# Matmul steps of 512 + 256 columns become three products of 256 columns, but for the opening step of each output block

## The chip, the cores and the metric

The kernel runs on one core of a Trainium2 chip. The metric is the device time of one execution in microseconds (us), as the median of several runs. The profile is one execution of its own, recorded by the hardware profiler.

## The reference

One layer of a streaming encoder over a sequence of 256 tokens of width 2048, all in float32. Every large product in it has the 256 tokens on one side and a weight matrix on the other:

```python
u = rms_norm(h, norm_mix[l])
proj = u @ w_in[l]
...
h = h + jnp.concatenate([o_dn.astype(h.dtype), o_mla.astype(h.dtype)], axis=-1) @ w_out[l]
h = h + memory_cross_attention(rms_norm(h, norm_xattn[l]), mem_n, xa_wq[l],
                               xa_wk[l], xa_wv[l], xa_wo[l])
h = h + conv_ffn(rms_norm(h, norm_ffn[l]), ffn_w_up[l], ffn_conv[l],
                 ffn_conv_bias[l], ffn_w_down[l])
```

`w_in` feeds a delta-rule head group and a latent-attention head group; `w_up` has 2 x 5632 columns, `w_down` 5632 rows. A final normalisation follows.

## The kernel before

Activations lie with features on the 128 partitions and the 256 tokens (T = 256) along the free axis. To keep float32 accuracy with the cheaper `fp32r` matmul, each operand is split into a high and a low part. An activation tile holds `[x_hi | x_lo]` side by side in 512 columns; a weight tile is loaded by DMA (`raw`), ScalarE writes its high part `wh` (L102) and VectorE the low part `wl` (L103). One k step adds to a block of 128 output features what 128 input features give: `wh·x_hi`, `wh·x_lo` and `wl·x_hi`.

`kstep` (L116 to L122) makes a k step of two matmuls: `wh` by all 512 columns into a whole PSUM bank (L122), so that `wh·x_lo` collects in columns 256 to 511, and `wl` by 256 columns into the lower half (L120). Every other step turns the two around, so that the stream on TensorE reads 512, 256, 256, 512, 512, 256, 256, 512 and so on. When a block is done, `halves` (L140, L141) or `add_res` adds the two halves of the bank.

`kstep3` (L125 to L127) makes the same step of three matmuls of 256 columns, all into the lower half. It serves the query projection of the cross-attention (`xa_wq`, tile `xq`), the block products of the latent attention (tile `lath`), the scores and mixes of the cross-attention (tiles `kh`, `qh`, `pTx`, in the PSUM tiles `psa` and `psb`), and the last block of `w_down`. The change leaves it as it is.

`kstep` makes 3460 k steps. By the tile that it reads:

- `u`: 39 blocks of 16 steps of the input projection (the first in the program);
- `om` and `od`: the two halves of the output projection, 16 blocks of 8 steps each;
- `mh`: 16 blocks of 16 steps for the keys of the cross-attention;
- `xo`: 16 blocks of 16 steps of its output projection;
- `fx`: 88 blocks of 16 steps of `w_up`;
- `ga` and `gb`: 15 blocks of 44 steps of `w_down` (a sixteenth is made with `kstep3`).

In the first 406 us `fill(n)` draws n steps of `u` or `om` at a time between the small float32 matmuls of the two attention groups. From `od` on, the blocks follow one another on TensorE with few other matmuls between them (`rstd_col` and `rstd_row`, the `v_block` of 512-column products, scores and mixes). TensorE's order is that of the code; the other engines are ordered by a scheduler.

Of the kernel before, what the change touches and what calls it, by code (L numbers as in the profile page):

```python
# [22 lines left out]
T = 256  # L23
# [47 lines left out]
def trunk(ctx, tc, a):  # L71
    nc = tc.nc
    V, S, PE = nc.vector, nc.scalar, nc.tensor
# [8 lines left out]
    def psg():  # L82
        return pg.tile([P, 512], F32, name="psg", tag="psg")

    def psa(tag="a"):
        return pa.tile([P, 512], F32, name="ps" + tag, tag=tag, bufs=1 if tag == "c" else 2)
# [19 lines left out]
    def load_w(src, n=1024, pieces=1):  # L106
        raw = wpool.tile([P, 1024], F32, name="raw", tag="raw")
        nc.sync.dma_start(raw[:, 0:n], src)
        return split_w(raw, n, pieces)

    turn_ = [False]

    def kstep(ps, wh, wl, xh2, first, last):
        rev = turn_[0] and not first  # L116
        turn_[0] = not rev
        for lo in ((True, False) if rev else (False, True)):
            if lo:
                PE.matmul(ps[:, 0:256], wl, xh2[:, 0:256], start=False, stop=last, skip_group_check=True)  # L120
            else:
                PE.matmul(ps[:, 0:512], wh, xh2, start=first, stop=last, skip_group_check=True)  # L122

    def kstep3(ps, wh, wl, xh2, first, last):
        PE.matmul(ps[:, 0:T], wh, xh2[:, 0:T], start=first, stop=False)  # L125
# [3 lines left out]
    def gemm_block(w, nb, x, step=kstep):  # L129
        ps = psg()  # L130
        for hf in range(2):
            wh, wl = load_w(w[2 * nb + hf])
            for j in range(8):
                k = 8 * hf + j
                step(ps, wh[:, j * P:(j + 1) * P], wl[:, j * P:(j + 1) * P], x(k), k == 0, k == KC - 1)
        return ps
# [29 lines left out]


    def rstd_col(*accs):
        ps = psa("c")
        for t in range(2):  # L170
            for i, acc in enumerate(accs):
                PE.matmul(ps[:, t:t + 1], acc[:, t * P:(t + 1) * P], ones[:, 0:1], start=i == 0,
                          stop=i == len(accs) - 1)
        r = small.tile([P, 2], F32, name="rcol", tag="rcol", bufs=2)
        S.activation(r, ps[:, 0:2], AF.Sqrt, scale=1.0 / D, bias=eps)
        V.reciprocal(r, r)
        return r

    def rstd_row(col):
        ps = psa("c")  # L180
        for t in range(2):
            PE.matmul(ps[:, t * P:(t + 1) * P], col[:, t:t + 1].to_broadcast([P, P]), idn, start=True, stop=True)
        r = small.tile([P, T], F32, name="rrow", tag="rstd", bufs=2)
        S.copy(r, ps[:, 0:T])
        return r
# [4 lines left out]
    with ExitStack() as ph:  # L190
# [11 lines left out]
        with tc.tile_pool(name="xpool", bufs=1) as xpl:  # L202
# [13 lines left out]
            for k in range(KC):  # L216
                wh, wl = w0[k // 8]
                j = k % 8
                kstep(ps0, wh[:, j * P:(j + 1) * P], wl[:, j * P:(j + 1) * P], u(k), k == 0, k == KC - 1)
# [49 lines left out]
        def drawn():  # L269
            ready = {0: lead}  # L270
            ps = None
            i = 0
            while i < len(queue):
                for n in range(i, min(i + 1 + ahead[0], len(queue))):
                    if n not in ready:
                        ready[n] = load_w(queue[n][0], pieces=2)
                _, x, begin, first, last, done = queue[i]
                if begin:
                    begin()
                wh, wl = ready.pop(i)  # L280
                if first:
                    ps = psg()
                for j in range(8):
                    kstep(ps, wh[:, j * P:(j + 1) * P], wl[:, j * P:(j + 1) * P], x(j),
                          first and j == 0, last and j == 7)
                    if last and j == 7:
                        done(ps)
                    pos[0] += 1
                    for at_, f in [t for t in later if t[0] <= pos[0]]:
                        later.remove((at_, f))  # L290
                        f()
                    yield
                i += 1
# [3 lines left out]
        gen = drawn()  # L297

        def fill(n):
            for _ in range(n):  # L300
                next(gen, None)

        def until(n):
            fill(n - pos[0])
# [66 lines left out]
        with ExitStack() as ms:  # L371
# [20 lines left out]

            lats.append(latent)
            fill(8)
            rs0 = rstd_col(*accs)
            fill(6)
            rs.append(rstd_row(rs0))
            latent(0, ps0)
            latent(1, ps1)
            until(Q0 + 8)  # L400
            ps = psa()
# [72 lines left out]
            ps = psa()  # L474
# [5 lines left out]
            ps = psa()  # L480
# [22 lines left out]
            def w_mla(i):  # L503
                c = order.index(i)
                for n in order[c:c + 2]:
                    if n not in wm:
                        wm[n] = load_w(a["w_mla"][n])
                return wm[i]
# [63 lines left out]
            for i in range(2):  # L572
                kn = mp.tile([P, 4, T], F32, name="kn", tag="kn")
                wh, wl = w_mla(i)
                for n in range(4):
                    ps = psg()
# [8 lines left out]
                wh, wl = w_mla(2 + i)  # L585
                for t in range(2):
                    ps = psg()
# [325 lines left out]
    with ExitStack() as ph:  # L913
# [4 lines left out]
        for n in range(KC):  # L918
            wh, wl = load_w(a["w_out"][2 * n + 1])
            ps = psg()  # L920
# [15 lines left out]
        for n in range(KC):  # L936
            ps = gemm_block(a["xa_wk"], n, mh)
            if n == 0:
                rmc = rstd_col(macc)
                psk = ps  # L940
            else:
                if n == 1:
                    rsm = rstd_row(rmc)
                    normed(psk, rsm, kT[:, 0])
                normed(ps, rsm, kT[:, n])
            split_gain(xq(n), hT[:, n], sm[:, C_XA + n:C_XA + n + 1])
            accum_sq(xacc, hT[:, n], n == 0)
# [80 lines left out]
        for n in range(3):  # L1028
            v_block(n)
            if n == 0:  # L1030
                rcx = rstd_col(xacc)
            elif n == 1:
                rsx = rstd_row(rcx)
# [23 lines left out]
        for n in range(KC):  # L1057
            if n < 3:
                ps = pw[n]
            else:  # L1060
                ps = psg()
# [10 lines left out]
    with ExitStack() as ph:  # L1072
# [39 lines left out]
        for n in range(KC):  # L1112
            ps = psg()
            for c in range(6):
                nk = 8 if c < 5 else 4
                o = n * NF * P + c * 1024
                wh, wl = load_w(a["w_down"][n, :, c * 1024:c * 1024 + nk * P], nk * P)
# [131 lines left out]
```

## Time and profile before

| what | value |
| --- | --- |
| median of 3 runs | 1580.1 us (1579.47 to 1580.53) |
| time of the profiled execution | 1580.7 us |
| its span in the trace | 1578.9 us |
| TensorE (PE) busy | 1546.1 us, 98% of the span |
| weight loads (PEld), which overlap PE | 1358.5 us, 86% |
| VectorE (DVE) busy | 1119.3 us, 71% |
| ScalarE (ACT) busy | 889.3 us, 56% |
| DMA | mean 179 GB/s |

The profiled execution's time is its span and 1.8 us around it. Matmuls overlap: a 256-column matmul is shown as lasting 0.28 us, but the next starts after some 0.11 to 0.12 us. The price of a matmul in a stream is therefore the distance from its start to the next start, not its duration.

### The profile page before, as it was taken

To read this page: it belongs to the slowest core of one execution; us is meant where nothing else is said; L and a number is where in the kernel's file an instruction comes from. 1 tells how busy PE (TensorE), PEld (TensorE's weight loads), DVE (VectorE), ACT (ScalarE), POOL (GpSimd) and SP (SyncE) were. 2 spreads that over 40 slices of the span, in tenths; PEclk is the share of its full clock that TensorE was granted. 3 is DMA by queue.
4 is the path that set the end of the run, shared out by engine and by line. 5 is a ranking of instruction groups with operands and counts; after the bars stand their busy time and mean duration, and the time that the engine had idled before them with its cause. 6 is when DMAs were issued, how large, how long until landed. Compare 5 with 4: busy or idle time off the path is not lost.

```text
span 1578.9 us, 24577 instructions
## 1 busy us (share of the span) xinstructions
PE 1546.1 (98%) x9386; PEld 1358.5 (86%) x9386; DVE 1119.3 (71%) x1810; ACT 889.3 (56%) x1473; POOL 147.9 (9%) x152
## 2 busy tenths in 40 slices
PE   7999999999999999999999999999999999999996
PEld 5887877888888889999888888888888888888886
DVE  8687688696976555566777888878888886445453
ACT  7867666757764444455556666556665665344441
POOL 2224021001320000000110000000000000111112
PEclk9999999999999999999999999999999999999998
DMA  7564443364665555544555555555555556666663
GB/s 248 179 214 141 144 134 126 118 214 132 200 200 189 191 188 193 174 161 133 174 188 187 187 189 190 194 188 189 192 193 187 187 190 183 190 190 183 198 187 106
DMA packets 80773, 282.22 MB, mean 179 GB/s; under 512 B 9392, under 2 KB 10304, under 8 KB 80656
## 3 DMA queue, kind: packets, MB, share of 16 engines
q1 hardware_dynamic: 79344, 277.86, 54.3%
q0 software_dynamic: 1312, 2.80, 0.6%
q8 instruction: 73, 1.20, 0.3%
q14 instruction: 44, 0.36, 0.1%
HBM read 277.83 MB, written 2.11 MB: 177 GB/s over the span
## 4 chain that ended last, share of the span: by engine, by line
PE 88%; DVE 5%; ACT 4%; issue 1%; DMA 1%; SPq 0%; DVEq 0%; ACTq 0%
PE psg L122 46%; PE psg L120 23%; PE psg L125 3%; PE psg L126 3%; PE psg L127 3%; PE psg L960 2%; PE psg L959 2%; PE psg L958 2%; DVE wl L103 2%; ACT wh L102 1%; DMA raw<-in_w_out_dram 1%; PE psa L620 0%; PE psa L539 0%; DVE qkv L330 0%; DVE hT L1132 0%
## 5 line engine op out<-in xcount | busy, mean ns | idle before, releaser
L103 DVE TENSOR_TENSOR wl<-raw,wh 128x1024 fp32r<-128x1024 f32 (+2 forms) x614 | 647.3, 1061 | 286.1 <-ACT wh L102 279.2
L102 ACT CAST wh<-raw 128x1024 fp32r<-128x1024 f32 (+2 forms) x614 | 550.8, 909 | 401.5 <-PE psg L122 243.2
L122 PE MATMUL psg<-fx,wh 128*128 128x512 f32 x1408 | 439.8, 393 | 0.0
L120 PEld LDWEIGHTS psg<-fx,wl 128*128 128x128 f32 x1408 | 264.7, 188 | 60.0
L120 PE MATMUL psg<-fx,wl 128*128 128x256 f32 x1408 | 277.6, 279 | 0.0
L122 PE MATMUL psg<-u,wh 128*128 128x512 f32 x624 | 207.7, 404 | 8.9 <-DVE u L149 8.2
L122 PEld LDWEIGHTS psg<-fx,wh 128*128 128x128 f32 x1408 | 212.0, 188 | 0.0
L120 PEld LDWEIGHTS psg<-u,wl 128*128 128x128 f32 x624 | 119.3, 192 | 29.3 <-DVE wl L103 3.1
L140 ACT COPY half<-psg 128x256 f32<-128x256 f32 x143 | 53.2, 372 | 154.9 <-PE psg L122 154.7
L120 PE MATMUL psg<-u,wl 128*128 128x256 f32 x624 | 134.3, 289 | 1.7 <-DVE wl L103 1.7
L122 PE MATMUL psg<-gb,wh 128*128 128x512 f32 x420 | 133.4, 393 | 0.0
L122 PEld LDWEIGHTS psg<-u,wh 128*128 128x128 f32 x624 | 99.3, 191 | 12.5 <-DVE u L149 9.0
L120 PEld LDWEIGHTS psg<-gb,wl 128*128 128x128 f32 x420 | 79.0, 188 | 17.9
L1089 DVE SCALAR_TENSOR_TENSOR y<-ub,sm,y 128x256 f32<-128x256 f32 x176 | 84.7, 482 | 3.5 <-ACT y L1087 0.3
L120 PE MATMUL psg<-gb,wl 128*128 128x256 f32 x420 | 82.8, 278 | 0.0
L122 PE MATMUL psg<-mh,wh 128*128 128x512 f32 x256 | 80.5, 394 | 0.0
L122 PE MATMUL psg<-xo,wh 128*128 128x512 f32 x256 | 80.4, 393 | 0.0
L141 DVE TENSOR_TENSOR ub<-psg,half 128x256 f32<-128x256 f32 x88 | 37.4, 425 | 60.1 <-ACT half L140 60.1
L122 PE MATMUL psg<-ga,wh 128*128 128x512 f32 x240 | 77.3, 393 | 0.0
L125 PE MATMUL psg<-xq,wh 128*128 128x256 f32 x256 | 71.2, 278 | 0.0
L126 PE MATMUL psg<-xq,wh 128*128 128x256 f32 x256 | 70.9, 277 | 0.0
L127 PE MATMUL psg<-xq,wl 128*128 128x256 f32 x256 | 70.9, 277 | 0.0
(405 smaller groups left out, 2411.3 us busy)
## 6 DMA issues: line engine op xcount, KB each, us to landing
raw<-in_w_up_dram SPq DMA_DIRECT2D x176, 512.0 KB, 3.4
raw<-in_w_down_dram SPq DMA_DIRECT2D x80, 512.0 KB, 4.2
raw<-in_w_in_dram SPq DMA_DIRECT2D x77, 512.0 KB, 3.9
raw<-in_w_out_dram SPq DMA_DIRECT2D x32, 512.0 KB, 4.2
raw<-in_xa_wk_dram SPq DMA_DIRECT2D x32, 512.0 KB, 3.5
raw<-in_xa_wv_dram SPq DMA_DIRECT2D x32, 512.0 KB, 3.5
raw<-in_xa_wq_dram SPq DMA_DIRECT2D x32, 512.0 KB, 3.4
raw<-in_xa_wo_dram SPq DMA_DIRECT2D x32, 512.0 KB, 3.4
```

The lines of the kernel that those rows point to most:

```text
L102: S.copy(wh[:, c], raw[:, c])
L103: V.tensor_sub(wl[:, c], raw[:, c], wh[:, c].bitcast(F32))
L120: PE.matmul(ps[:, 0:256], wl, xh2[:, 0:256], start=False, stop=last, skip_group_check=True)
L122: PE.matmul(ps[:, 0:512], wh, xh2, start=first, stop=last, skip_group_check=True)
L125: PE.matmul(ps[:, 0:T], wh, xh2[:, 0:T], start=first, stop=False)
L126: PE.matmul(ps[:, 0:T], wh, xh2[:, T:2 * T], start=False, stop=False)
L127: PE.matmul(ps[:, 0:T], wl, xh2[:, 0:T], start=False, stop=last)
L140: S.copy(t, ps[:, T:2 * T])
L141: V.tensor_add(out, ps[:, 0:T], t)
L958: PE.matmul(pss[t], xh, wh[:, wk], start=(k == 0), stop=False)
L959: PE.matmul(pss[t], xh, wl[:, wk], start=False, stop=False)
L1089: V.scalar_tensor_tensor(y, b[:, j:j + T], sm[:, cw + j:cw + j + 1], y, ALU.mult, ALU.add)
```

## The change

`kstep` no longer alternates. A step that opens a block (`first`), and a step that comes right after `rstd_col`, `rstd_row` or the start of a `fill` (the flag `wide`), is made of 512 + 256 columns, in that order. Every other step is three products of 256 columns, all into the lower half of the bank, as in `kstep3`.

```diff
-    turn_ = [False]
+
+    wide = [True]
 
     def kstep(ps, wh, wl, xh2, first, last):
-        rev = turn_[0] and not first
-        turn_[0] = not rev
-        for lo in ((True, False) if rev else (False, True)):
-            if lo:
-                PE.matmul(ps[:, 0:256], wl, xh2[:, 0:256], start=False, stop=last, skip_group_check=True)
-            else:
-                PE.matmul(ps[:, 0:512], wh, xh2, start=first, stop=last, skip_group_check=True)
+        if first or wide[0]:
+            PE.matmul(ps[:, 0:512], wh, xh2, start=first, stop=last, skip_group_check=True)
+        else:
+            PE.matmul(ps[:, 0:T], wh, xh2[:, 0:T], start=False, stop=False, skip_group_check=True)
+            PE.matmul(ps[:, 0:T], wh, xh2[:, T:2 * T], start=False, stop=False, skip_group_check=True)
+        wide[0] = False
+        PE.matmul(ps[:, 0:T], wl, xh2[:, 0:T], start=False, stop=last, skip_group_check=True)
...
     def rstd_col(*accs):
+        wide[0] = True
...
     def rstd_row(col):
+        wide[0] = True
...
         def fill(n):
+            wide[0] = True
             for _ in range(n):
```

The instructions on PE where a block of `w_up` opens, in the steady part of the program, before (each row is a matmul, out<-activation tile, weight tile, with the semaphores that it waits for; x2 stands for two in a row):

```order
L122 MATMUL psg<-fx_8477,wh 128x512 [waits Activation_49]
L120 MATMUL psg<-fx_8477,wl 128x256 [waits DVE_49]
L120 MATMUL psg<-fx_8477,wl 128x256
L122 MATMUL psg<-fx_8477,wh 128x512 x2
L120 MATMUL psg<-fx_8477,wl 128x256 x2
```

The same place with the change, where L118 is the wide product, L120 and L121 are `wh·x_hi` and `wh·x_lo`, and L123 is `wl·x_hi`:

```order
L123 MATMUL psg<-fx_9687,wl 128x256
L118 MATMUL psg<-fx_9686,wh 128x512 [waits DVE_49,Activation_49]
L123 MATMUL psg<-fx_9686,wl 128x256 [waits DVE_49]
L120 MATMUL psg<-fx_9686,wh 128x256
L121 MATMUL psg<-fx_9686,wh 128x256
L123 MATMUL psg<-fx_9686,wl 128x256
```

A block of 16 steps was 32 matmuls and is now 47, with one 512-column product in it, and the wide product that opens most blocks waits for two engines instead of one.

The instructions on PE in the latent attention of the first 406 us, where a `fill` of two or three steps lies between float32 products (L553 and L558, later L557 and L562), before:

```order
L122 MATMUL psg<-u_77,wh 128x512 [waits Activation_49]
L120 MATMUL psg<-u_77,wl 128x256 [waits DVE_49]
L553 MATMUL psc<-cg,s 128x128 [waits DVE_49] x2
L553 MATMUL psc<-cg,s 128x128
L120 MATMUL psg<-u_77,wl 128x256
L122 MATMUL psg<-u_77,wh 128x512 x2
L120 MATMUL psg<-u_77,wl 128x256
L558 MATMUL psb<-pT,vm 128x256 [waits Activation_49]
```

and with the change:

```order
L120 MATMUL psg<-u_77,wh 128x256 [waits Activation_49]
L121 MATMUL psg<-u_77,wh 128x256
L123 MATMUL psg<-u_77,wl 128x256 [waits DVE_49]
L557 MATMUL psc<-cg,s 128x128 [waits DVE_49] x2
L557 MATMUL psc<-cg,s 128x128
L118 MATMUL psg<-u_77,wh 128x512
L123 MATMUL psg<-u_77,wl 128x256
L120 MATMUL psg<-u_77,wh 128x256
L121 MATMUL psg<-u_77,wh 128x256
L123 MATMUL psg<-u_77,wl 128x256
L562 MATMUL psb<-pT,vm 128x256 [waits Activation_49]
```

The steps stay where they were between the float32 products; the first step after them opens wide, the next is three products. In all, the program goes from 6920 matmuls in `kstep` to 10094 (286 wide products, 3174 steps of three, and the 286 low products that go with the wide ones): 3174 matmuls and 3174 weight loads more.

## Rows read from the trace of the kernel before

**Rows 1.** The page: busy time and share of each engine, then the final chain.

```profile
PE 1546.1 (98%) x9386; PEld 1358.5 (86%) x9386; DVE 1119.3 (71%) x1810; ACT 889.3 (56%) x1473; POOL 147.9 (9%) x152
...
PE 88%; DVE 5%; ACT 4%; issue 1%; DMA 1%; SPq 0%; DVEq 0%; ACTq 0%
```

**Rows 2.** Windows: stretch, length, busy PE, PEld, DVE, ACT, POOL; clock, DMA, GB/s.

```profile
16.00:406.00 390.00, 378.54 (x2420) 325.37 (x2420) 305.06 (x636) 272.29 (x579) 73.68 (x78) 0.99 0.49 159
...
837.00:1325.00 488.00, 488.00 (x2820) 428.04 (x2819) 396.49 (x616) 296.70 (x444) 0.00 (x0) 1.00 0.58 189
```

**Rows 3.** Timeline of PE in `w_up`: start, length, instruction; 100 double steps apart.

```profile
900.00 0.62 PE L122 MATMUL psg<-fx,wh 128*128 128x512 f32 x2
...
969.34 0.62 PE L122 MATMUL psg<-fx,wh 128*128 128x512 f32 x2
```

**Rows 4.** Timeline of PE, four query blocks: entry, then the last of 192 products.

```profile
606.75 0.28 PE L125 MATMUL psg<-xq,wh 128*128 128x256 f32 x1
...
607.46 0.28 PE L125 MATMUL psg<-xq,wh 128*128 128x256 f32 x1
...
628.43 0.28 PE L127 MATMUL psg<-xq,wl 128*128 128x256 f32 x1
```

**Rows 5.** Timeline of PE, last `w_down` block: entry, then the last of 132 products.

```profile
1548.96 0.39 PE L122 MATMUL psg<-gb,wh 128*128 128x512 f32 x1
1549.19 0.28 PE L125 MATMUL psg<-ga,wh 128*128 128x256 f32 x1
1549.31 0.28 PE L126 MATMUL psg<-ga,wh 128*128 128x256 f32 x1
...
1564.62 0.28 PE L127 MATMUL psg<-gb,wl 128*128 128x256 f32 x1
```

**Rows 6.** Timeline of PE: a 512 product between 256s in the latent attention.

```profile
112.73 0.39 PE L122 MATMUL psg<-u,wh 128*128 128x512 f32 x1
112.95 0.40 PE L120 MATMUL psg<-u,wl 128*128 128x256 f32 x2
113.19 0.63 PE L122 MATMUL psg<-u,wh 128*128 128x512 f32 x2
```

**Rows 7.** Timeline of PE: score products, then a 512 product of `xo`.

```profile
737.77 0.28 PE L126 MATMUL psa<-kh,qh 128*128 128x256 f32 x1
...
738.97 0.28 PE L127 MATMUL psa<-kh,qh 128*128 128x256 f32 x1
739.09 0.40 PE L122 MATMUL psg<-xo,wh 128*128 128x512 f32 x1
739.32 0.40 PE L120 MATMUL psg<-xo,wl 128*128 128x256 f32 x2
739.56 0.63 PE L122 MATMUL psg<-xo,wh 128*128 128x512 f32 x2
```

**Rows 8.** Timeline of PE: the end of 24 `lath` products, then 512s and 256s.

```profile
126.72 0.39 PE L122 MATMUL psg<-u,wh 128*128 128x512 f32 x1
126.96 0.39 PE L120 MATMUL psg<-u,wl 128*128 128x256 f32 x2
127.19 0.62 PE L122 MATMUL psg<-u,wh 128*128 128x512 f32 x2
```

**Rows 9.** Timeline of PE: 144 query products behind four float32 products.

```profile
659.05 0.60 PE L1007 MATMUL psc<-cg,sx 128*128 128x128 f32 x4
659.40 0.37 PE L125 MATMUL psg<-xq,wh 128*128 128x256 f32 x1
...
659.73 0.28 PE L127 MATMUL psg<-xq,wl 128*128 128x256 f32 x1
...
675.71 0.28 PE L127 MATMUL psg<-xq,wl 128*128 128x256 f32 x1
```

**Rows 10.** Instructions of line 122: PE's queue, and those of `od`.

```profile
L122 PE MATMUL psg<-od,wh x128: 388/395/473, 405.8 to 450.0; 128*128 128x512 f32 x128
L122 PEldq EVENT_SEMAPHORE  x31: 51/51/51, 12.7 to 761.7; - x31
```

## Prediction

> **What bounds the kernel now.** I read the page first: PE is busy 98% of the span and holds 88% of the chain that ended last [rows 1]. The windows by stage say where it is not: from 16 to 406 us PE stands for 390.00 − 378.54 = 11.5 us, while in the 488 us of `w_up` it never stands and VectorE, the next busiest, works 396.49 us [rows 2]. The granted clock there is 1.00, the 2.4 GHz level. So outside the first stage the time is the number of matmuls times their distance, and the distance is what I have to read, from the timelines of PE.
>
> In `w_up` 100 double steps take 969.34 − 900.00 = 69.34 us [rows 3], 693.4 ns for two k steps: **346.7 ns a step** of today's form. The step of three products of 256 columns is in the trace too, and it has not one price:
>
> - Four query blocks, 192 products: the first six take 0.71 us (118 ns each), the other 185 distances 628.43 − 607.46 = 20.97 us, 113.4 ns each [rows 4]. That is **340 ns a step**.
> - The last `w_down` block, 132 products: 1564.62 − 1549.19 = 15.43 us over 131 distances, 117.8 ns each [rows 5]: **353.4 ns a step**, from the first product to the last.
> - Score products: 738.97 − 737.77 = 1.20 us over ten, 120 ns each [rows 7]: 360 ns a step.
>
> Today's step lies between the first two, 6.7 ns from either. The sign of the change hangs on which pace the new stream falls into. Both hold for over a hundred products, in the same kind of tiles, with the same clock, so I call them the fast and the slow pace and ask what sets them.
>
> **What sets the pace.** The products of the last block follow a single 512-column product: 1548.96 to 1549.19 is 0.23 us, then 0.12, and the slow pace stays to the end [rows 5]. A 512 product that comes out of fast `lath` products does the same: 0.22 us, then two products in 0.24 us [rows 6]. That is just what each block of the new kernel begins with: one 512 product, then 256s only (46 of them in a block of 16 steps). So I expect the first block to run slowly, and ask what the next 512 product does, which comes out of slow 256s. The nearest case is 739.09: out of score products at 120 ns, the 512 takes 0.23 us and the two 256s behind it 0.24 us together [rows 7], slow again. Another case goes the other way: behind 24 `lath` products, a 512 at 126.72 takes 0.24 us and its two 256s 0.23 us [rows 8]. Those 24 are eight whole steps of three. The new blocks hold 46, 22 or 130 products of 256 between two wide ones (16, 8 or 44 steps), one more than whole steps each time, so a block's end is not the place of 126.72, and I put it with 739.09. I take the slow pace as the likeliest.
>
> Products that start behind float32 matmuls find the fast pace: after one distance of 0.21 us, 659.73 to 675.71 holds 141 distances of 113.3 ns [rows 9]. The changed kernel puts a wide product at those places, and the few three-product steps that stand directly behind it I take as fast: 225 steps in the first stage and 91 later, counted in the order.
>
> **The sum.** From `od` on there are 128 + 256 + 256 + 1408 + 660 = 2708 steps. 91 are fast: 91 × −6.7 = −0.6 us. The other 2617 cost 6.7 ns more each: three products at 117.8 ns, and a wide step about the same (0.23 to 0.24 us [rows 7, 8] and 0.118): +17.4 us. Together +16.8 us. The first stage has 752 steps: 225 fast ones give −1.5 us and the rest at most +3.5 us; some of these lie beside the 11.5 us for which PE waits anyway. Bounds −1.5 and +3.5; I take +1.2, near the middle.
>
> The rest costs nothing. The 3174 further weight loads lie under the matmuls, as the three loads of a step do in [rows 4] at 340 ns. The PSUM bank is read by the same `halves` and `add_res`. No DMA is issued more or elsewhere. The second semaphore of the wide product becomes an instruction of PE's queue of 51 ns [rows 10]; some 97 more of them could cost 97 × 0.051 = 4.9 us if nothing covered them. Today they stand before each of the 16 `od` blocks, whose 128 steps take 44.2 us between the first and the last wide product, 348 ns a step [rows 10]: at most 1.3 ns a step above the pace, 0.2 us for 16. So I take 0 for it, and 4.9 as the upper bound. Weights are needed later than before, not sooner, so DVE and ACT (396 and 297 of 488 us) gain slack.
>
> Sum: +16.8 + 1.2 = +18.0 us on the profiled execution, 1580.7 to 1598.7. The median of the runs stands 0.6 us below that execution: **1598 us**. Its own range is 1592 to 1605, by the first stage, the extra waits and blocks that find the fast pace.
>
> **Against a rule.** A step costs one more matmul, and one can ask for a fixed price per matmul. From [rows 3] it would be 693.4 ns less the 640 ns in which 1536 columns pass at 2.4 GHz, over four: 13.3 ns. The new step would then take 360 ns, +42 us, which the 340 ns of [rows 4] rule out for an undisturbed stream. The Trainium skill, "TensorE: Matmul & The Clock Gate", section "Back-to-back issue gap", gives a warm gap of N/2.4 + 2.5 ns, a fixed 2.5 ns. By that, an estimate, the step grows by 2.5 ns and the kernel by 7.9 us, to 1588. No row here agrees with it: 256 columns stand at 113 to 120 ns and not at 109, and the price of one shape changes with its neighbours. The trace decides.
>
> **The rivals.**
>
> - *The fast pace everywhere* (the other side). The wide product costs 0.22 to 0.23 us [rows 5, 6] and the 256s run at 113.4 ns. For it speak the query blocks, which enter from a row of 512 products and fall into the fast pace after six products [rows 4], with the same k step. Against it: those 512 products form a stream of their own, and the single one of [rows 5, 6] is followed by the slow pace. Price: 2708 × −6.7 = −18.1 us and up to −5 us in the first stage, of which waits hide half: about 1560 us. It decides as soon as the distance behind the 512 in `w_up` is 113 and not 118.
> - *Blocks take turns.* A slow block's 512 leads to a fast block as at 126.72 [rows 8], a fast block's 512 to a slow one [rows 6]. Half the steps at +6.7, half at −6.7: about 1580 us, no change. That a block's 256s are not whole steps speaks against it, but this is read from a handful of places.
> - *A slower pace still*, the 120 ns of the score products [rows 7]: 2708 × 13.3 = +36 us, about 1616 us. Those write other PSUM tiles and read other tiles; the last block reads `ga` and `gb`, as 660 of the steps do, and has 117.8.
> - *One small price for each further matmul*, whatever its neighbours, that puts the new step halfway between today's and the slow one: 2708 × 3.35 = +9 us, about 1589 us. The two prices of the same step in [rows 4, 5] speak against it. (The page's rule comes out there too.)
>
> **How the numbers follow.** Slow pace 0.66; fast pace 0.17; turns 0.11; 120 ns 0.02; a small fixed price 0.04. A measurement of this kernel can tell 0.2%, 3.2 us, from no change. Slower: 0.66 + 0.02 + 0.04 = 0.72. The turns give no change, but a few fast or slow blocks more would leave that band: 0.09 same, 0.01 to either side. Faster 0.17 + 0.01 = 0.18, slower 0.73. The likeliest gives 1598. The range reaches down to the case of turns and leaves the fast pace and the 120 ns out: 1578 to 1606.
>
> **What would show it.** In the timeline of `w_up`: L118 to L123 0.23 to 0.24 us, then 0.12 us from product to product and no 0.11 within a block; a block of 16 steps in 5.65 us against 5.55 now. The 88 blocks should grow by 1408 × 6.7 ns = 9.4 us, the 15 of `w_down` by 4.4, `od` by 0.8. PE stays busy through these stages; its queue holds about a hundred more semaphore instructions without a gap at a block's start. I am wrong if the products behind L118 stand 0.113 us apart, in all blocks (1560) or in every second (1580), or if a wait of VectorE or ScalarE opens a gap at the blocks' starts.

## The result, and the profile after

The changed kernel takes **1598.4 us** (median; 1598.16 to 1601.63 in four runs) against 1580.2, a ratio of 1.012 [1.0103, 1.0138]. It is slower by 18.2 us; 18 were forecast, by a slower pace of the same columns.

The page, busy time and the final chain, against [rows 1]:

```profile
PE 1567.2 (98%) x12560; PEld 1517.2 (95%) x12560; DVE 1119.3 (70%) x1810; ACT 874.4 (55%) x1473; POOL 134.2 (8%) x152
...
PE 89%; DVE 6%; ACT 3%; issue 1%; DMA 1%; SPq 0%; DVEq 0%; ACTq 0%
```

TensorE makes 3174 matmuls more and is busy 21 us longer; VectorE works as long as before. The windows of the first stage, of `w_up` and of `w_down`, as in [rows 2]:

```profile
16.00:406.00 390.00, 378.22 (x3002) 353.77 (x3003) 303.10 (x631) 267.88 (x575) 71.47 (x78) 0.99 0.48 158
...
839.00:1336.90 497.90, 497.90 (x4146) 493.81 (x4145) 392.51 (x613) 282.21 (x442) 0.96 (x1) 1.00 0.57 186
1337.00:1568.00 231.00, 231.00 (x1949) 230.30 (x1948) 114.26 (x124) 94.39 (x109) 22.31 (x27) 1.00 0.62 187
```

In the two large stages PE never waits, and the granted clock of 1.00 is the upper level of 2.4 GHz, as before. So the time lost there is pace. The timeline of PE shows it; a block of `w_up` from one wide product (L118) to the next:

```profile
924.29 0.40 PE L118 MATMUL psg<-fx,wh 128*128 128x512 f32 x1
924.53 0.28 PE L123 MATMUL psg<-fx,wl 128*128 128x256 f32 x1
924.65 0.28 PE L120 MATMUL psg<-fx,wh 128*128 128x256 f32 x1
924.77 0.28 PE L121 MATMUL psg<-fx,wh 128*128 128x256 f32 x1
...
929.83 0.28 PE L123 MATMUL psg<-fx,wl 128*128 128x256 f32 x1
929.95 0.40 PE L118 MATMUL psg<-fx,wh 128*128 128x512 f32 x1
```

The wide product takes 0.24 us and the 256s 0.12 us each; the block takes 929.95 − 924.29 = 5.66 us where 16 steps of [rows 3] take 16 × 346.7 ns = 5.55. That is the entry of the last block in [rows 5], in all blocks of `w_up` but the second and the third, which stand behind float32 matmuls and run fast.

The first starts of each stage on PE, read from both traces (us):

| stage | its length before | after | difference | forecast |
| --- | --- | --- | --- | --- |
| to the first `om` | 340.74 | 340.87 | +0.13 | |
| `om` | 65.04 | 67.92 | +2.88 | +1.2 with the row above |
| `od` | 44.46 | 45.30 | +0.84 | +0.8 |
| `mh` | 89.65 | 90.93 | +1.28 | +1.7, less fast steps |
| values, queries, scores | 199.20 | 200.19 | +0.99 | 0 |
| `xo` | 92.29 | 93.80 | +1.51 | +1.7, less fast steps |
| `w_up` (`fx`) | 489.01 | 497.98 | +8.97 | +9.4, less fast steps |
| `w_down` to the last matmul | 247.35 | 251.75 | +4.40 | +4.4 |

From `od` on that is +18.0 us, with +16.8 forecast. The profiled execution took 1601.63 us, some 3 us above the three others, and `om` shows why: this window of 10 us has PE waiting for 2.04 us, and a granted clock of 0.83, so that part of it ran at the 1.2 GHz level:

```profile
350.00:360.00 10.00, 7.96 (x54) 7.67 (x53) 5.08 (x9) 3.25 (x6) 0.00 (x0) 0.83 0.47 159
```

The same stretch of before had 9.37 us of PE and a clock of 1.00. If that makes the 3 us, `om` and what lies ahead of it give about nothing, and the +18.2 of the median is the +18.0 from `od` on. This is argued and not shown, as the other executions have no trace.

### The profile page after: what moved, and what is told of

It reads as the page before. It is cut to its first block, busy times and chain, and to the rows that moved or that the text cites. A ratio compares the mean times of both kernels' runs of the same rounds, so it can differ in the third digit from the quotient of the medians.

```text
span 1599.9 us, 31093 instructions
## 1 busy us (share of the span) xinstructions
PE 1567.2 (98%) x12560; PEld 1517.2 (95%) x12560; DVE 1119.3 (70%) x1810; ACT 874.4 (55%) x1473; POOL 134.2 (8%) x152
## 4 chain that ended last, share of the span: by engine, by line
PE 89%; DVE 6%; ACT 3%; issue 1%; DMA 1%; SPq 0%; DVEq 0%; ACTq 0%
PE psg L123 23%; PE psg L121 22%; PE psg L120 22%; PE psg L118 4%; PE psg L128 3%; PE psg L127 3%; PE psg L126 3%; DVE wl L103 2%; PE psg L964 2%; PE psg L963 2%; PE psg L962 2%; ACT wh L102 1%; DMA raw<-in_w_out_dram 1%; DVE qkv L334 1%; PE psa L624 1%
## 5 line engine op out<-in xcount | busy, mean ns | idle before, releaser
L123 PE MATMUL psg<-fx,wl 128*128 128x256 f32 x1408 | 395.5, 281 | 0.0
L121 PE MATMUL psg<-fx,wh 128*128 128x256 f32 x1320 | 370.8, 281 | 0.0
L120 PE MATMUL psg<-fx,wh 128*128 128x256 f32 x1320 | 370.7, 281 | 0.0
L123 PEld LDWEIGHTS psg<-fx,wl 128*128 128x128 f32 x1408 | 264.2, 188 | 0.0
L120 PEld LDWEIGHTS psg<-fx,wh 128*128 128x128 f32 x1320 | 253.0, 192 | 4.1
L121 PEld LDWEIGHTS psg<-fx,wh 128*128 128x128 f32 x1320 | 247.8, 188 | 0.0
L123 PE MATMUL psg<-u,wl 128*128 128x256 f32 x624 | 177.0, 284 | 1.9 <-DVE wl L103 1.9
L120 PE MATMUL psg<-u,wh 128*128 128x256 f32 x517 | 147.3, 285 | 1.1 <-ACT wh L102 0.8
L121 PE MATMUL psg<-u,wh 128*128 128x256 f32 x517 | 146.4, 283 | 0.4 <-DVE u L150 0.4
L123 PEld LDWEIGHTS psg<-u,wl 128*128 128x128 f32 x624 | 119.5, 192 | 3.0 <-DVE wl L103 2.8
L120 PE MATMUL psg<-gb,wh 128*128 128x256 f32 x420 | 118.0, 281 | 0.0
L121 PE MATMUL psg<-gb,wh 128*128 128x256 f32 x420 | 118.0, 281 | 0.0
L123 PE MATMUL psg<-gb,wl 128*128 128x256 f32 x420 | 118.0, 281 | 0.0
L120 PEld LDWEIGHTS psg<-u,wh 128*128 128x128 f32 x517 | 99.9, 193 | 6.7 <-ACT wh L102 1.0
L121 PEld LDWEIGHTS psg<-u,wh 128*128 128x128 f32 x517 | 98.7, 191 | 1.3 <-DVE u L150 0.8
L120 PEld LDWEIGHTS psg<-gb,wh 128*128 128x128 f32 x420 | 80.6, 192 | 0.0
L121 PEld LDWEIGHTS psg<-gb,wh 128*128 128x128 f32 x420 | 78.8, 188 | 0.0
L123 PEld LDWEIGHTS psg<-gb,wl 128*128 128x128 f32 x420 | 78.8, 188 | 0.0
L123 PE MATMUL psg<-xo,wl 128*128 128x256 f32 x256 | 71.9, 281 | 0.0
```

The source lines that it names most:

```text
L120: PE.matmul(ps[:, 0:T], wh, xh2[:, 0:T], start=False, stop=False, skip_group_check=True)
L121: PE.matmul(ps[:, 0:T], wh, xh2[:, T:2 * T], start=False, stop=False, skip_group_check=True)
L123: PE.matmul(ps[:, 0:T], wl, xh2[:, 0:T], start=False, stop=last, skip_group_check=True)
```

## The experiments

The theory: the pace of a stream of 256s is set where it is entered and lasts; a single 512 leaves the slow pace, which means that what follows it runs slowly. The main rival: each further matmul has a price of its own. Lines below are changes to `kstep` or its callers.

**Two 512s in a row.** The low product of a block's first step is held back behind the 512 of the second step:

```diff
-        if first or wide[0]:
+        if first or held or wide[0]:
...
         wide[0] = False
+        if first:
+            held.append((ps, wl, xh2))
+            return
+        if held:
+            p0, w0_, x0 = held.pop()
+            PE.matmul(p0[:, 0:T], w0_, x0[:, 0:T], start=False, stop=False, skip_group_check=True)
```

> Each block opens with two 512 products in a row, then their two low products, and goes on with three products of 256; everything else is as in the changed kernel. Theory (the pace is set by how the stream of 256s is entered, and lasts): 512, 512, 256, 256 is the double step of the kernel before, whose second 256 is followed at 113 ns, so the 256s behind it find the fast pace of 340 ns a step. From od on 302 steps at 346.7 and 2406 at 340 ns: 2406 x 6.7 = 16 us less than before, about 1563 us. Rival (each further matmul has its price, whatever stands beside it): 151 of some 3000 further pairs of matmuls are saved, so about 1597 us, as the changed kernel.

Measured: **1563.7 us**, ratio 0.9898 [0.9877, 0.9919]. The timeline of PE at the opening of a block of `w_up`:

```profile
904.84 0.62 PE L120 MATMUL psg<-fx,wh 128*128 128x512 f32 x2
905.30 0.28 PE L130 MATMUL psg<-fx,wl 128*128 128x256 f32 x1
905.42 0.28 PE L131 MATMUL psg<-fx,wl 128*128 128x256 f32 x1
905.53 0.28 PE L122 MATMUL psg<-fx,wh 128*128 128x256 f32 x1
905.65 0.28 PE L123 MATMUL psg<-fx,wh 128*128 128x256 f32 x1
905.76 0.28 PE L131 MATMUL psg<-fx,wl 128*128 128x256 f32 x1
```

Behind the second low product the starts stand 0.11 to 0.12 us apart, 905.42 to 905.76 in three distances of 0.113. The kernel is 34.6 us faster than the changed one, with 202 matmuls fewer of 12560. The rival would have had to charge 0.17 us for each.

Behind float32 matmuls the pair does not always do this. The second and the third block of `w_up` stand behind `rstd_col` and `rstd_row`. Opened by a pair they run slowly here; opened by a single 512 they run fast in the changed kernel. The third block of this run, from its first 256 to the pair of the fourth:

```profile
839.66 0.28 PE L130 MATMUL psg<-fx,wl 128*128 128x256 f32 x1
...
844.84 0.63 PE L120 MATMUL psg<-fx,wh 128*128 128x512 f32 x2
```

5.18 us / 44 = 117.7 ns. The fourth block, whose pair comes out of this slow one, is fast. In `xo`, behind other float32 matmuls, one 512 and two both lead to the fast pace. So what is said of one or two 512s holds where they stand between 256s.

**No flag.** Only the step that opens a block is wide (the three `wide[0] = True` go).

> The changed kernel without the flag: only the step that opens a block is 512 + 256, a block that goes on behind other matmuls does so with three products. Theory: streams behind float32 matmuls find the fast pace in either form, so the time stays within 2 us of the changed kernel, about 1598 us. Rival (the wide step behind other matmuls hides a weight load there): 80 resumptions lose up to 0.1 us each, about 1606 us.

Measured: 1597.2 us, 1.0109 [1.0092, 1.0126]. The flag is worth nothing that can be told apart; the openings are what counts.

**The kernel before, not turned.** `for lo in (False, True)` in place of the alternation.

> The kernel before with the steps not turned around: 512, 256, 512, 256, no matmul more and no wait more. Theory (the place in the stream sets the price): a 512 behind a single 256 pays 0.235 us and the 256 behind it 0.118 us, as at the openings of the changed kernel, so 353 ns a step instead of 346.7 and 2708 x 6.7 = 18 us more: about 1598 us. Rival (the price hangs on the number of matmuls): 1580 us.

Measured: 1598.1 us, 1.0114 [1.0098, 1.0131]. The timeline of PE in `w_up`:

```profile
969.73 0.40 PE L119 MATMUL psg<-fx,wh 128*128 128x512 f32 x1
969.96 0.28 PE L117 MATMUL psg<-fx,wl 128*128 128x256 f32 x1
970.08 0.40 PE L119 MATMUL psg<-fx,wh 128*128 128x512 f32 x1
```

The 512 takes 0.23 us and the 256 behind it 0.12. The window of PE over 400 us of `w_up`:

```profile
900.00:1300.00 400.00, 400.00 (x2266) 1.00 0.57 186
```

That is 400 us / 1132 = 353 ns a step (a window counts two or three products more than start in it, as they overlap its edges), and 18 us more over the program, with not one matmul more. This rules the rival out from the other side: the neighbours set the price.

**Three products everywhere.** `kstep = kstep3`, and the evacuation reads the lower half alone.

```diff
-        S.copy(t, ps[:, T:2 * T])
-        V.tensor_add(out, ps[:, 0:T], t)
+        V.tensor_copy(out, ps[:, 0:T])
```

> Every step is three products of 256, the opening too, and the block is evacuated from the lower half of the bank alone (one VectorE copy instead of a ScalarE copy and an add, one add of a residual instead of two). Theory: no 512 product stands between the blocks, so a stream that starts behind float32 matmuls keeps the fast pace to its end; w_up from its second block on and all of w_down run at 340 ns a step: 1408 x 6.7 + 660 x 6.7 + 1.7 + 0.9 = 16 us less, with xo slow behind the scores (+1.7): about 1565 us. Rival (number of matmuls): 1599 us.

Measured: 1605.2 us, 1.0166 [1.0139, 1.0194]: **the expectation failed**. The timeline of PE behind `rstd_row` (L173), before the third block of `w_up`, and windows of PE alone (time, busy, count) of the block ahead of it and of `w_up` behind it:

```profile
860.21 0.50 PE L173 MATMUL psc<-cg,rcol 128*128 128x128 f32 x3
860.46 0.36 PE L116 MATMUL psg<-fx,wh 128*128 128x256 f32 x1
860.66 0.28 PE L117 MATMUL psg<-fx,wh 128*128 128x256 f32 x1
```

```profile
855.00:860.00 5.00, 5.00 (x47) 1.00 0.59 205
900.00:1300.00 400.00, 400.00 (x3399) 1.00 0.57 187
```

The block behind `rstd_col` runs at 5.00 us / 44 to 45, some 113 ns; then the stream is entered anew at 860.46 and runs at 400 us / 3397 = 117.8 ns, with no 512 in it, for 6239 distances to the end of `w_down`. That the pace lasts is right; that a stream behind float32 matmuls is always fast is wrong. The first stage lost time too: in this trace `od` starts at 418.62 us, 12.8 us later than in the kernel before. PE was busy 370.18 of the 390 us to 406 us, 8 us less than in the changed kernel, at a granted clock of 0.97 instead of 0.99. This execution took 1611.4 us, 6 more than the median.

**A tail of four float32 matmuls of one column** behind those of `rstd_row`, so that the entry looks like that behind `rstd_col`; and the same with a ScalarE copy ahead of the VectorE copy in the evacuation:

```diff
+        for t in range(4):
+            PE.matmul(ps[:, T + t:T + t + 1], idn, ones[:, 0:1], start=True, stop=True)
```

> All steps of three products, as in the run before it of that form, and rstd_row gets four float32 matmuls of one column behind its four of 128 (results unused), so that the stream behind it starts as it does behind rstd_col, where that run found the fast pace. Theory (the entry sets the pace, and a stream of 256s keeps it): the 671 distances of mh and 6239 of w_up and w_down that were slow become fast, 6910 x 4.4 ns = 30 us less than 1605, about 1575 us. Rival (a stream of 256s without a 512 falls into the slow pace whatever stands ahead): 1605 us and a little more.

> As the run with the four small matmuls, but a block is evacuated by a ScalarE copy and a VectorE copy behind it, so that the two engines have as many instructions there as in the kernel before. If the first stage of the all-three form (od starts 13 us later than before) lost its time to the evacuation, od starts near 406 us again and the time is about 1562 us. If it lost it to the paces and places of its matmuls, od stays late and the time is about 1575 us.

Measured: 1612.7 us, 1.0207 [1.0179, 1.0236] and 1605.5 us, 1.0154 [1.0132, 1.0176]. Neither theory fits. `w_up` stayed slow in both, but the 671 distances of `mh` behind the same tail were slow in the first and fast in the second. Windows of PE over 75 us of them, the first run and then the second:

```profile
477.50:552.50 75.00, 75.00 (x639) 1.00 0.53 184
```

```profile
473.50:548.50 75.00, 75.00 (x664) 1.00 0.55 191
```

About 117.8 and 113.3 ns, with the same matmuls ahead of them in the same order. So it is not the kind of matmul ahead of an entry that decides, but something finer, which these runs don't show.

A pace can also change within a stream of 256s alone. In `od` of the first of these runs the fast pace ended at one longer distance, 0.24 us from 432.64 to 432.88, with no other kind of matmul near. Windows of PE ahead of it and behind it:

```profile
420.00:431.00 11.00, 11.00 (x99) 1.00 0.67 227
434.00:454.00 20.00, 20.00 (x172) 1.00 0.78 234
```

11 us / 97 = 113.4 ns, 20 us / 170 = 117.6.

With the ScalarE copy `od` starts at 415.7 us instead of 419.2, against 405.8 in the kernel before. That the copy brought these 3.4 us back is not shown: it is one trace of each, and the executions of either kernel lie 6 to 8 us apart. Where the rest of the first stage's loss went was not settled.

**Two wide steps, their 512s apart.** 512, 256, 256, 512, then threes:

```diff
+        if second[0]:
+            second[0] = wide[0] = False
+            PE.matmul(ps[:, 0:T], wl, xh2[:, 0:T], start=False, stop=False, skip_group_check=True)
+            PE.matmul(ps[:, 0:512], wh, xh2, start=False, stop=last, skip_group_check=True)
+            return
```

> Each block opens with two wide steps turned around, 512, 256, 256, 512, and goes on with three products: as many matmuls of each kind as in the run with two 512 products in a row, in another order. Theory (what stands directly ahead of the 256s sets the pace): they follow a single 512 and are slow, about 1597 us. Rival (two wide steps a block are what helps, by the matmuls saved): 1564 us as that run. The prediction's own sign (whole steps of 256s between two 512s lead to the fast pace; here 42, fourteen whole steps) would give 1564 us too, or 1580 if blocks take turns.

Measured: 1591.4 us, 1.0071 [1.0052, 1.0090]: none of the three expected times, but between them. The windows of PE, 60 us of `xo` and 60 us of `w_up`:

```profile
766.00:826.00 60.00, 60.00 (x507) 1.00 0.55 193
860.00:920.00 60.00, 60.00 (x491) 1.00 0.54 184
```

The same order of matmuls, with 42 products of 256 between the openings in both, and yet 3% fewer in `w_up`. In `xo` the blocks from 761 us on run at 113 ns behind their opening, in `w_up` all behind the first at 117.8. The entries of one block each, `w_up`'s first, which is still fast, and a later one:

```profile
831.39 0.39 PE L125 MATMUL psg<-fx,wh 128*128 128x512 f32 x1
831.61 0.28 PE L130 MATMUL psg<-fx,wl 128*128 128x256 f32 x1
831.73 0.28 PE L121 MATMUL psg<-fx,wl 128*128 128x256 f32 x1
831.85 0.39 PE L122 MATMUL psg<-fx,wh 128*128 128x512 f32 x1
832.08 0.28 PE L127 MATMUL psg<-fx,wh 128*128 128x256 f32 x1
...
899.73 0.39 PE L125 MATMUL psg<-fx,wh 128*128 128x512 f32 x1
899.96 0.28 PE L130 MATMUL psg<-fx,wl 128*128 128x256 f32 x1
900.07 0.28 PE L121 MATMUL psg<-fx,wl 128*128 128x256 f32 x1
900.19 0.39 PE L122 MATMUL psg<-fx,wh 128*128 128x512 f32 x1
900.41 0.28 PE L127 MATMUL psg<-fx,wh 128*128 128x256 f32 x1
```

Coming out of the fast pace the opening takes 0.22, 0.12, 0.12, 0.23 us and leads to the fast pace; out of the slow one 0.23, 0.11, 0.12, 0.22 and to the slow one. From `od` on, where no float32 matmul stands in between, this opening hands on the pace that it finds at 143 of 144 places. The other one lies in `xo`, at 760.31: out of 72 products at the slow pace the opening takes 0.23, 0.12, 0.12, 0.23 us and leads to the fast pace. Windows of PE ahead of it and behind it:

```profile
751.90:760.20 8.30, 8.30 (x73) 1.00 0.37 128
761.30:765.70 4.40, 4.40 (x41) 1.00 0.59 223
```

So more than the pace ahead counts, and it is not known what. Two wide steps are not what helped in the first experiment; that their 512s stood in a row is.

**A pair, then no 512 at all.** The first experiment, with `kstep3` in `w_up` from the fifth block on and in all of `w_down`, and one VectorE operation to evacuate:

```diff
-            halves(ps, b[:, 2:2 + T])
-            V.tensor_mul(b[:, 2:2 + T], b[:, 2:2 + T], rsf)
+            if f < 2:
+                halves(ps, b[:, 2:2 + T])
+                V.tensor_mul(b[:, 2:2 + T], b[:, 2:2 + T], rsf)
+            else:
+                V.tensor_mul(b[:, 2:2 + T], ps[:, 0:T], rsf)
```

> The run with two 512 products in a row, but w_up from its third pair of blocks on and all of w_down are three products throughout, without any 512, evacuated from the lower half alone. Theory: the pace found at the second pair of blocks lasts to the end; 84 blocks of w_up and 15 of w_down save 2 x 6.7 ns each, 1.3 us: about 1562 us. Rival (a stream without 512s does not hold the fast pace for thousands of products): 1564 to 1592 us, by where it falls out.

Measured: **1562.5 us**, 0.9889 [0.9872, 0.9906], the lowest median of all versions, though too near the 1563.7 us of the first experiment to be told apart from it. The window of PE over 690 us:

```profile
850.00:1540.00 690.00, 690.00 (x6091) 1.00 0.58 192
```

690 us / 6089 = 113.3 ns. The three-product stream that crept for 735 us in the run of that form keeps the fast pace to its end here: the same kind of matmuls, entered in another way. And the program has 12556 matmuls, four fewer than the changed kernel, and is 36 us faster.

**One 512 in that stream, and a pair behind it.** The 45th block of `w_up` opens with one step of 512 + 256; in the second run the 67th opens with a pair besides:

```diff
+        wide_at = {(22, 0): one_wide, (33, 0): kstep}
...
-            pu = [gemm_block(a["w_up"], 2 * f, fx, step)]
+            pu = [gemm_block(a["w_up"], 2 * f, fx, wide_at.get((f, 0), step))]
```

> The fastest run so far (w_up from its third pair of blocks on and w_down without any 512), with one change: the 45th of the 88 blocks of w_up opens with a single step of 512 + 256, as every block of the changed kernel does. One matmul less in the whole program. Theory (a single 512 out of the fast pace leaves the slow pace, which lasts): 46 + 43 x 48 + 16 x 132 = 4222 products behind it go from 113.3 to 117.8 ns, 18.8 us more, about 1581 us, the slow pace from that block to the end of w_down. Rival (the pace belongs to the stretch or to the whole program's mix, not to one place): 1562.5 us.

> The same with a second change: the 67th block of w_up opens with two 512 products in a row. Theory (a pair of 512s leaves the fast pace out of either): slow from the 45th to the 66th block only, 46 + 21 x 48 = 1054 products, 4.7 us more than the run without a 512, about 1567 us. Rival (once slow, such a stream is reset by float32 matmuls alone): 1581 us.

Measured: 1581.1 us (1.0010 [1.0000, 1.0019] of before) and 1567.3 us (0.9923 [0.9909, 0.9938]). Against 1562.5 that is +18.5 and +4.8, with 18.8 and 4.7 expected. (The kernel before stood at 1579.0 us beside these two and at 1580.2 beside the other; the traces, from the first product of `w_up` to the last matmul, give +18.8 and +5.1.) The first run's timeline of PE at the 512 (L140), then its windows of PE before it and behind it:

```profile
1068.45 0.28 PE L136 MATMUL psg<-fx,wl 128*128 128x256 f32 x1
1068.57 0.39 PE L140 MATMUL psg<-fx,wh 128*128 128x512 f32 x1
1068.79 0.28 PE L144 MATMUL psg<-fx,wl 128*128 128x256 f32 x1
1068.91 0.28 PE L142 MATMUL psg<-fx,wh 128*128 128x256 f32 x1
```

```profile
868.00:1068.00 200.00, 200.00 (x1768) 1.00 0.58 195
1070.00:1270.00 200.00, 200.00 (x1701) 1.00 0.56 187
1400.00:1540.00 140.00, 140.00 (x1191) 1.00 0.63 186
```

One matmul less, and 18.5 us more: 0.22 us behind the 512, then 0.12 for the 4222 products that are left, into `w_down` (140 us / 1189 = 117.7 ns). The second run's windows of PE, before the 512, between it and the pair, and behind the pair:

```profile
868.00:1068.00 200.00, 200.00 (x1767) 1.00 0.59 193
1071.00:1190.00 119.00, 119.00 (x1013) 1.00 0.57 187
1200.00:1400.00 200.00, 200.00 (x1767) 1.00 0.62 193
```

119 us / 1011 = 117.7 ns between them, 113.3 on either side. Both ways of the switch are shown by one edit each.

**All traces together.** From `od` on, every place where one of these openings alone stands between two streams of ten or more 256s, over all runs:

| opening | out of the fast pace | out of the slow pace |
| --- | --- | --- |
| one 512 | slow behind it, 6 of 6 | slow, 284 of 284 |
| two 512s in a row | fast, 265 of 265 | fast, 15 of 15 |
| 512, 256, 256, 512 | fast, 30 of 30 | slow, 113 of 114 |

In the first stage, with waits and other matmuls close by, the first row is no rule: there three single 512s of the changed kernel led from the slow pace to the fast one (at 76.75, 102.51 and 129.13 us).

## Why the prediction was right, point by point

- **A single 512 out of the fast pace leaves the slow one.** Shown: one such 512 turned 4222 products slow. Reading it from [rows 5, 6] was enough.
- **The slow pace then goes through the block's end.** It does, in the changed kernel (5.66 us a block). The reason that I gave, that 46 products are not whole steps, is not settled. For it speaks the run with the 512s apart: behind 42 slow products, which are whole steps, the first 512 (899.73) is followed by two 256s in 0.23 us, as at 126.72 in [rows 8], and the second 512 takes 0.22 us, as one out of the fast pace does [rows 6]. The pace may thus have changed twice within that opening, but two products are too few to show it. Against it stands the 512 at 765.52 in the changed kernel, which comes behind 72 slow products, whole steps too, and leaves the slow pace.
- **+6.7 ns a step.** Shown by the table: `w_up` and `w_down` grew by 13.4 us, 13.8 forecast less the fast steps.
- **Streams behind float32 matmuls are fast.** Wrong as a rule, drawn from [rows 9]: behind such matmuls four blocks of `mh` and `w_up` and one stretch of `xo` run fast in the changed kernel, 67 steps of threes instead of the 91 I took, and in the all-three form the entry at 860.46 went the other way. In the sum this term was too favourable by 24 × 13.4 ns = 0.32 us. (The other term has a slip: 2617 × 6.7 ns is 17.5 us, not 17.4.)
- **What the change doesn't touch costs nothing.** Not quite: values, queries and scores took 0.99 us more. Their streams are entered otherwise. Windows of PE in the changed kernel, over queries as in [rows 9]:

```profile
665.40:675.40 10.00, 10.00 (x88) 1.00 0.58 195
```

  10 us / 85 to 86, some 117 ns, where [rows 9] had 113.3. The 512s of the first value block changed too: 20 us of them hold 87 in the changed kernel (from 546 us) and 89 before (from 541). These streams and the fast steps make about the 1.2 us between the +16.8 forecast and the +18.0 measured from `od` on. By the medians, if the rest was as in the trace, the first stage gave some 0.2 us instead of the +1.2 taken. That the sum came out at 18 to a few tenths is luck: two misses of about 1 us each cancelled.
- **The further semaphores cost nothing.** The changed kernel has them:

```profile
L118 PEldq EVENT_SEMAPHORE  x127: 51/51/51, 67.3 to 1334.9; - x127
```

  127 instead of the 31 of [rows 10], and PE is busy 497.90 of 497.90 us in `w_up`. The wide product behind one stands where the pace puts it.
- **Against a fixed price.** Two kernels with the same matmuls lie 18 us apart (the kernel before and the one not turned), two with 12560 and 12556 lie 36 us apart. That settles it. The Trainium skill, "TensorE: Matmul & The Clock Gate", section "Back-to-back issue gap", gives N/2.4 + 2.5 ns for an isolated matmul and says itself that in a stream of weight loads and matmuls both set the spacing. By its 2.5 ns the kernel would have taken 1588 us, an estimate; it took 1598.4, and the 256s stand at 113.3 or 117.8 ns where that formula has 109.

The rival of the fast pace (1560 us) was one step of the code away: the same openings with their 512s in a row give 1563.7.

Open is what the two paces are made of: what differs in the machine between 113.3 and 117.8 ns, and what picks one at an entry behind float32 matmuls, behind a wait or at the one odd opening of `xo`. Shown are that the paces last and the two switches between 256s.

## What to carry to other kernels

Where TensorE never waits, read the distance from start to start, for each shape and each neighbour: the same three products cost 340 or 353 ns here, and a mean over the program hides which. A stream of equal matmuls can hold a pace for hundreds of microseconds that was set by one or two instructions at its start, so look at the entry, and try the order of a few matmuls there before changing the form of all of them. Let the timeline of the real stream decide: a stretch of the wished-for form elsewhere in the program shows what can be, not what will be.

## What was not expected of the hardware

- Two paces of one stream, 113.3 and 117.8 ns for a 256-column product, each of which lasted over 6000 products (6239 slow, some 6090 fast) without falling out, while in `od` of one run the fast one ended at a single longer distance of 0.24 us.
- A single 512-column product in the fast stream cost 18.5 us behind it; two in a row ended the slow pace. Behind `rstd_col` and `rstd_row` it was the other way round: fast behind one, slow behind two.
- The opening 512, 256, 256, 512 handed on either pace at 143 of 144 places: 60 us held 507 matmuls in one stage and 491 in another, in the same order.
